# Weight-ring tiles 32 bytes longer, in a two-layer decoder trunk with PEER retrieval

## The chip, the cores and the metric

One core of a Trainium2 chip runs the whole program. The metric is the device time of one execution in microseconds (us); the time of the kernel before is the median of three runs.

## The reference, cut to what matters

512 tokens of width 1024 go through two layers. Each layer is a mixer (gated linear attention in the first, stick-breaking attention in the second, both beside attention into 256 memory tokens), an output projection, a layer norm, then the PEER block and another layer norm. The PEER block takes most of the time:

```python
q = (xf @ w_q).reshape(N, PEER_HEADS, 2, PEER_QHALF)
s = jnp.einsum('nhpd,hpkd->nhpk', q, subkeys)
# two rounds of top-16 give 128 of 16384 experts a token, and gates g
act = jax.nn.gelu(jnp.einsum('nd,nhkd->nhk', xt, u_tab[it]), approximate=False)
out = jnp.einsum('nhk,nhkd->nd', gt * act, v_tab[it])
```

## The kernel before, in words

**Precision.** Every fp32 operand of a projection is split into two tiles of type fp32r, a high part `hi` (a copy on ACT, L93) and the rest `lo` (a subtraction on DVE, L94). A product is then three matmuls. In `stat_mm` (L105 to L115) the weight block is the stationary operand and the activations `xhi`, `xlo` move: L113 is hi with xhi, L114 hi with xlo, L115 lo with xhi, for each of eight chunks of 128 rows. In `mov_mm` (L241 to L248) it is the other way round: the weight block moves, 512 columns at a time, past a stationary block of 128 x 128; L244, L246 and L248 each issue two matmuls.

**The PEER block** (`peer`, L943 on) has two long stages. For 384 of the 512 tokens all 16384 experts are computed densely; the other 128 tokens take their 128 experts by gathers.

- Stage 1 (L1336 to L1366; about 375 to 940 us, and 1880 to 2450 us in the second layer): for each of 128 blocks of `peer_u`, a DMA of 512 KB into `ur`, the split into `uh` and `ul`, 24 matmuls of 384 columns into `ph`, and a Gelu. Beside them run the selection of the experts on DVE (`Sel`), the one-hot gate matmuls into `pg` (L1259, L1260), the gathers of rows of `peer_u` on POOL's queue and their products on DVE (L1022).
- Stage 2 (L1420 to L1433; about 945 to 1440 us, and 2460 to 2950 us): for each of 128 blocks of `peer_v`, a DMA into `vr`, the split into `vh` and `vl`, the gate-weighted activation `w` (L1408) and its split into `whi` and `wlo` (L1411, L1412), and 18 matmuls of 512 columns into six accumulators: for each of three groups of 128 tokens, twice whi with vh, twice whi with vl, twice wlo with vh. Beside them run the gathers of `peer_v` and their sums on DVE (L1040).

Ahead of stage 1 the queries `pq` (16 blocks, L1310 to L1332) are made by `stat_mm` too. In both stages the order of work on PE, DVE and ACT is that of the program text (`manual_schedule`), and the side work is dealt out to the blocks by written costs in ns (`WB`, `GU`, `GR` and the others).

**Rings.** `split` takes its tiles from the pool `E.hl` (L59), three buffers of `hi` and three of `lo`, each 128 x 1024 fp32r, 4096 bytes in a partition. The raw blocks come from a ring of four (`RB`), and their loads are issued on SP's queue. `whi` and `wlo` have five buffers each (`TAIL`, L1406, L1407), 1536 bytes in a partition. Buffers of one name lie one behind the other, and the pools lie one behind the other in the order in which they are opened: const, xres, raw, hl, lnp, and then the pools of each part.

**Where the tiles lie.** In the compiled program of before, the byte at which a tile starts in its partition, modulo 128, is:

| tiles | start modulo 128 |
|---|---|
| `xhi`, `xlo` (pool xres, ahead of hl) | 64 |
| the six of hl (`uh`, `ul`, `vh`, `vl`, `anh` and the others): 87744, 91840, 95936 for hi, 100032, 104128, 108224 for lo | 64 |
| `whi` and `wlo`, ten tiles from 166336 on | 64 |
| `mhl`, the split memory tokens (mixer A) | 0 |
| mixer A's output projection: `woh`, `wol`, and `cat` but for chunks 4 and 5 | 96 |
| the same, chunks 4 and 5, which lie in `xhi` and `xlo` | 64 |
| mixer B's output projection, all of it | 64 |

All slices of these tiles that a matmul reads begin at multiples of 512 bytes.

Of the kernel before, what the change touches and what calls it, by code (L numbers as in the profile page):

```python
# [10 lines left out]
F32R = mybir.dt.float32r  # L11
# [5 lines left out]
P = 128  # L17
T = 512
NT = 4
D = 1024  # L20
# [10 lines left out]
def new_x(E):  # L31

    E.xhi = E.xp.tile([P, NC, T], F32R, tag="xhi", name="xhi")
    E.xlo = E.xp.tile([P, NC, T], F32R, tag="xlo", name="xlo")


def setup(ctx, tc):
# [19 lines left out]
    new_x(E)  # L57
    E.raw = ctx.enter_context(tc.tile_pool(name="raw", bufs=RB))
    E.hl = ctx.enter_context(tc.tile_pool(name="hl", bufs=3))  # L59
# [5 lines left out]
@contextmanager  # L65
def psum_pool(E, **tags):

    with E.tc.tile_pool(name="ps", bufs=1, space=bass.MemoryType.PSUM, reuse_waits="tile") as p:
        E.ps, old = (p, tags), getattr(E, "ps", None)
        yield  # L70
        E.ps = old


def psum(E, name="ps", tag="ps"):
    p, tags = E.ps
    return p.tile([P, 512], F32, tag=tag, name=name, bufs=tags[tag])


def load_raw(E, src, name):
    t = E.raw.tile([P, D], F32, tag="raw", name=name)  # L80
    E.last_load = E.nc.sync.dma_start(t, src)
    return t


def split(E, raw, name, pool=None, tag="", later=None, eng=None, rows=None):

    nc = E.nc
    eng = eng or nc.vector
    pool = pool or E.hl
    hi = pool.tile([P, D], F32R, tag=tag + "hi", name=f"{name}h")  # L90
    lo = pool.tile([P, D], F32R, tag=tag + "lo", name=f"{name}l")
    if rows is None:
        nc.scalar.activation(hi, raw, AF.Copy)  # L93
        sub = lambda: eng.tensor_sub(lo, raw, hi.bitcast(F32))  # L94
    else:
        nc.scalar.activation(hi, raw, AF.Copy, scale=rows)
        sub = lambda: eng.scalar_tensor_tensor(lo, raw, rows, hi.bitcast(F32), op0=ALU.mult, op1=ALU.subtract)
    if later is None:
        sub()
    else:  # L100
        later.append(sub)
    return hi, lo
# [525 lines left out]
def mixer_b(E, wst, wnat, wo, lng, lnb):  # L628
# [5 lines left out]
    with tc.tile_pool(name="bcat", bufs=1, reuse_waits="tile") as cp:  # L634
# [8 lines left out]
        with tc.tile_pool(name="mbx", bufs=1, reuse_waits="tile") as mp, tc.tile_pool(name="mbwk", bufs=2, reuse_waits="tile") as wk:  # L643
# [20 lines left out]
            def ev_stat(b, ps):  # L664
                if b >= 12:
                    dst = qm[:, b - 12]
                else:
                    dst = wk.tile([P, T], F32, tag=("kT", "qT")[b % 2], name="kq", bufs=1)
                    kq[b] = dst
                act.append(nc.scalar.activation(dst, ps, AF.Copy))  # L670
# [113 lines left out]
            with psum_pool(E, ps=2, z=4, c=2), tc.manual_schedule(engines={eng.PE, eng.DVE, eng.Activation}):  # L784
                parts = {}

                def prep(src, b):

                    raw = load_raw(E, src[b], "bs")
                    hi = E.hl.tile([P, D], F32R, tag="hi", name="bsh")  # L790
                    lo = E.hl.tile([P, D], F32R, tag="lo", name="bsl")
                    nc.scalar.activation(hi, raw, AF.Copy)
                    nc.gpsimd.tensor_sub(lo, raw, hi.bitcast(F32))
                    parts[b] = hi, lo

                def stat(b):
                    ps = psum(E, name="bsp")
                    stat_mm(E, ps, *parts.pop(b))
                    ev_stat(b, ps)

                vacc = []

                def values(u):

                    hi, lo = parts.pop(4 + u)
                    if u == 0:
                        vacc.extend(psum(E, name="bva") for _ in range(2))
                    for cc in range(4):
                        c = 4 * u + cc
                        h, l = hi[:, cc * 256:(cc + 1) * 256], lo[:, cc * 256:(cc + 1) * 256]  # L810
                        for t in range(NT):
                            xh, xl = E.xhi[:, c, t * P:(t + 1) * P], E.xlo[:, c, t * P:(t + 1) * P]
                            a = vacc[t // 2][:, t % 2 * 256:t % 2 * 256 + 256]
                            nc.tensor.matmul(a, xh, h, start=(c == 0 and t % 2 == 0), stop=False, skip_group_check=True)
                            nc.tensor.matmul(a, xh, l, start=False, stop=False, skip_group_check=True)
                            nc.tensor.matmul(a, xl, h, start=False, stop=(c == NC - 1), skip_group_check=True)

                prep(wst, 4)
                prep(wst, 5)
                for j in range(1, 6):  # L820
                    h, g = 2 * j, 2 * j - 2
                    phase1(h)
                    ln(h)
                    ln(h + 1)
                    phase3(g)
                    phase3(g + 1)
                    softplus(h)
                    softplus(h + 1)
                    if j < 5:
                        stat(h + 2)  # L830
                    else:
                        values(0)
                    sp_hi(h)
                    sp_hi(h + 1)
                    if j < 4:
                        prep(wst, h + 4)
                    elif j == 4:
                        prep(wnat, 4)
                    if j < 5:
                        stat(h + 3)  # L840
                    else:
                        values(1)
                        for k in range(2):
                            nc.scalar.activation(v[:, 2 * k:2 * k + 2, 512:], vacc[k].rearrange("p (t n) -> p t n", t=2), AF.Copy)
                    sp_lo(h)
                    sp_lo(h + 1)
                    if j < 4:
                        prep(wst, h + 5)
                    elif j == 4:
                        prep(wnat, 5)  # L850
                    phase4(j - 1)
                phase3(10)
                phase3(11)
                phase4(5)
# [58 lines left out]
TD = 384  # L913
# [23 lines left out]
LEAD = 3  # L937
TAIL = 5
RB = 4
SEG = [(0, 1, 0, 16, 16), (1, 1, 16, 8, 8), (2, 1, 24, 8, 5), (3, 1, 32, 8, 4), (4, 1, 40, 4, 3), (5, 3, 44, 4, 2), (8, 8, 56, 1, 1)]  # L940


def peer(E, mixer, wq, sk, ut, vt, un, lng, lnb, out_dram=None):  # L943
# [6 lines left out]
    with ExitStack() as pp:  # L950
# [97 lines left out]
        with ExitStack() as up:  # L1048
# [21 lines left out]
            class Sel:  # L1070
# [18 lines left out]
                def stage2(self, h):  # L1089

                    v = self.top_s[:, 2 * h:2 * h + 4].rearrange("p (h two) k -> p two h k", two=2)
                    for a, n, o, w, m in SEG:
                        dst = cand[:, :, o:o + n * w].rearrange("p h (a w) -> p h a w", a=n)[:, :, :, :m]
# [219 lines left out]
            for r in range(17):  # L1313
                if r < 16:
                    if r < LEAD:
                        pn = pes[r]
                    else:
                        hi, lo = parts.pop(r)
# [17 lines left out]
            for b in range(P + 1):  # L1336
# [7 lines left out]
                if b < P:  # L1344
                    if b > 0:
                        prep(b + 18, later)
                    hi, lo = parts.pop(16 + b)
# [22 lines left out]
        wv = pp.enter_context(tc.tile_pool(name="wv", bufs=2, reuse_waits="tile"))  # L1370
# [14 lines left out]
        def vprep(i):  # L1385
            if i >= P:
                return
            b = vorder[i]
            raw = load_raw(E, vt[b * P:(b + 1) * P], "vr")
            if i in gcuts:  # L1390
                g1 = gcuts[gcuts.index(i) + 1]
                if i == 0:
                    vp["g"] = g0
                else:
                    vp["g"] = E.xp.tile([P, NSUB, g1 - i, TS], F32, tag=("xhi", "xlo")[gcuts.index(i) % 2], name="gl")
                nc.sync.dma_start(vp["g"], Gd[:, :, b:b + g1 - i].rearrange("s p i n -> p s i n"))
                vp["i"] = i
            if b >= KB:
                av = keep[:, b - KB]
            else:  # L1400
                if b % AL == 0:
                    vp["a"] = wv.tile([P, AL, TD], F32, tag="al", name="al", bufs=3)
                    nc.sync.dma_start(vp["a"].rearrange("p (g a) n -> p g a n", a=AB), Ad[b // AB:b // AB + AL // AB].rearrange("g p a n -> p g a n"))
                av = vp["a"][:, b % AL]
            w = wv.tile([P, TD], F32, tag="w", name="w")
            whi = wv.tile([P, TD], F32R, tag="whi", name="whi", bufs=TAIL)  # L1406
            wlo = wv.tile([P, TD], F32R, tag="wlo", name="wlo", bufs=TAIL)  # L1407
            nc.vector.tensor_mul(w.rearrange("p (s n) -> p s n", s=NSUB), vp["g"][:, :, i - vp["i"]],  # L1408
                                 av.rearrange("p (s n) -> p s n", s=NSUB))
            hi, lo = split(E, raw, "v", wv if i >= P - (TAIL - 3) else None)  # L1410
            nc.scalar.activation(whi, w, AF.Copy)  # L1411
            nc.vector.tensor_sub(wlo, w, whi.bitcast(F32))  # L1412
            vp[i] = (whi, wlo, hi, lo)

        tail = []
        with tc.manual_schedule(engines={mybir.EngineType.DVE, mybir.EngineType.Activation, mybir.EngineType.PE}):
# [3 lines left out]
            for b in range(P):  # L1420
# [4 lines left out]
                whi, wlo, hi, lo = vp.pop(b)  # L1425
# [104 lines left out]
```

## Time and profile before

| | |
|---|---|
| median of 3 runs | 2988.55 us (2986.0 to 3000.78) |
| the profiled execution | 2996.65 us, its span 2994.9 us |
| granted TensorE clock, mean | 0.989 |
| PE busy | 2935.1 us (98% of the span), 16250 matmul records |
| weight loads (PEld) busy | 2591.7 us (87%) |
| DVE busy | 2401.1 us (80%) |
| ACT busy | 1428.3 us (48%) |
| POOL busy | 634.0 us (21%) |
| DMA | 789.91 MB, mean 264 GB/s |

Busy times are sums of the instructions' durations without overlap. Matmuls are pipelined, so the duration of one (342 ns for `ph`) is longer than the distance from its start to the next one's; the distances are read from the timeline. PEld is the queue of weight loads, which run beside matmuls.

### The profile page before, as it was taken

The page shows a single profiled execution, that of the slowest core. Times are in us where ns is not written, and L with a number is a line of the kernel's source. Part 1 is how long each engine was busy: PE and PEld are TensorE (multiplying, and loading weights), DVE is VectorE, ACT ScalarE, POOL GpSimd, SP SyncE. Part 2 cuts the span into 40 slices and gives each one's busy share as a digit, 9 for nine tenths or more (in the row PEclk, how much of TensorE's full clock was granted, in tenths as well). Part 3 has the DMA queues.
Part 4 walks back from the last instruction along what each step waited for, and adds up shares of the span by engine and source line. Part 5 has one row for each costly group of instructions (what it writes and reads, how often), then busy time and mean ns, then how long its engine had stood idle before and what let it go on. Part 6 is the DMA issues. An engine that isn't in the chain of part 4 may idle for free.

```text
span 2994.9 us, 44504 instructions
## 1 busy us (share of the span) xinstructions
PE 2935.1 (98%) x16250; PEld 2591.7 (87%) x16250; DVE 2401.1 (80%) x5301; ACT 1428.3 (48%) x2484; POOL 634.0 (21%) x560
## 2 busy tenths in 40 slices
PE   8999999999999999999999999999999999999998
PEld 7878899999998888888766788999999998888886
DVE  5555899999886888888856648999999778888888
ACT  5342357666674333333345513466676653333332
POOL 0100132221233222222002000321213233222220
PEclk9999999999999999999999989999999999999999
DMA  4331488889999999999411313789889999999995
GB/s 171 119 106 57 146 301 302 320 303 328 335 323 337 313 349 353 374 344 346 150 64 43 105 39 118 283 310 321 303 325 323 332 326 334 352 348 363 355 354 175
DMA packets 315131, 789.91 MB, mean 264 GB/s; under 512 B 41872, under 2 KB 134048, under 8 KB 308512
## 3 DMA queue, kind: packets, MB, share of 16 engines
q1 hardware_dynamic: 216960, 419.48, 41.0%
q0 software_dynamic: 73728, 268.47, 25.4%
q10 hardware_dynamic: 24224, 99.13, 8.4%
q8 instruction: 127, 2.08, 0.3%
q14 instruction: 92, 0.75, 0.1%
HBM read 692.09 MB, written 94.90 MB: 263 GB/s over the span
## 4 chain that ended last, share of the span: by engine, by line
PE 92%; DVE 5%; issue 1%; DMA 1%; ACT 1%; DVEq 0%; ACTq 0%; SPq 0%
PE ph L113 11%; PE acc L244 11%; PE acc L246 11%; PE ph L115 11%; PE ph L114 11%; PE acc L248 11%; PE pq L114 2%; PE pq L115 2%; PE pq L113 2%; PE pg L1259 1%; PE pg L1260 1%; PE pss L1307 1%; PE oacc L246 1%; PE oacc L248 1%; PE oacc L244 1%
## 5 line engine op out<-in xcount | busy, mean ns | idle before, releaser
L113 PE MATMUL ph<-xhi,uh 128*128 128x384 f32 x2048 | 701.4, 342 | 0.0
L115 PE MATMUL ph<-xhi,ul 128*128 128x384 f32 x2048 | 686.7, 335 | 0.2
L114 PE MATMUL ph<-xlo,uh 128*128 128x384 f32 x2048 | 686.0, 335 | 0.0
L93 ACT ACTIVATE vh<-vr 128x1024 fp32r<-128x1024 f32 x256 | 271.4, 1060 | 604.0 <-issue 455.8
L987 POOL DMA_INDIRECT gr<-in_un,gidx x256 | 302.7, 1182 | 1032.6 <-DVE gr L1022 807.4
L244 PE MATMUL acc<-vh,whi 128*128 128x512 f32 x1536 | 474.7, 390 | 8.3 <-ACT whi L1411 8.3
L246 PE MATMUL acc<-vl,whi 128*128 128x512 f32 x1536 | 474.5, 390 | 0.0
L248 PE MATMUL acc<-vh,wlo 128*128 128x512 f32 x1536 | 473.7, 390 | 0.4 <-DVE wlo L1412 0.4
L94 DVE TENSOR_TENSOR vl<-vr,vh 128x1024 fp32r<-128x1024 f32 x256 | 313.4, 1224 | 169.2 <-ACT vh L93 168.8
L987 POOL DMA_INDIRECT gr<-in_vt,gidx x256 | 279.8, 1093 | 773.5 <-DVE va L1040 664.0
L93 ACT ACTIVATE uh<-ur 128x1024 fp32r<-128x1024 f32 x288 | 304.6, 1058 | 245.8 <-PE ph L114 234.4
L94 DVE TENSOR_TENSOR ul<-ur,uh 128x1024 fp32r<-128x1024 f32 x288 | 350.4, 1217 | 74.2 <-ACT uh L93 72.7
L114 PEld LDWEIGHTS ph<-xlo,uh 128*128 128x128 f32 x2048 | 386.4, 189 | 0.0
L115 PEld LDWEIGHTS ph<-xhi,ul 128*128 128x128 f32 x2048 | 385.5, 188 | 0.9 <-DVE ul L94 0.9
L113 PEld LDWEIGHTS ph<-xhi,uh 128*128 128x128 f32 x2048 | 386.0, 188 | 0.0
L244 PEld LDWEIGHTS acc<-vh,whi 128*128 128x128 f32 x1536 | 288.0, 188 | 70.2 <-ACT whi L1411 10.8
L248 PEld LDWEIGHTS acc<-vh,wlo 128*128 128x128 f32 x1536 | 288.2, 188 | 61.6 <-DVE wlo L1412 2.0
L246 PEld LDWEIGHTS acc<-vl,whi 128*128 128x128 f32 x1536 | 288.3, 188 | 61.4 <-DVE vl L94 1.8
L1040 DVE SCALAR_TENSOR_TENSOR va<-gr,gw,va 128x1024 f32<-128x1024 f32 x254 | 325.1, 1280 | 12.6 <-DMA gr<-in_vt,gidx 12.4
L1022 DVE SCALAR_TENSOR_TENSOR gr<-gr,xnat 128x1024 f32<-128x1024 f32 x256 | 310.2, 1214 | 16.4 <-DMA gr<-in_un,gidx 16.4
L1232 ACT ACTIVATE obl<-obh,rat 128x128 f16<-128x128 f16 x768 | 244.3, 393 | 20.8 <-ACT gt L1263 5.2
L1411 ACT ACTIVATE whi<-w 128x384 fp32r<-128x384 f32 x256 | 130.7, 511 | 46.0 <-DVE w L1408 45.9
(332 smaller groups left out, 4165.0 us busy)
## 6 DMA issues: line engine op xcount, KB each, us to landing
ur<-in_ut SPq DMA_DIRECT2D x256, 512.0 KB
vr<-in_vt SPq DMA_DIRECT2D x256, 512.0 KB
Gd<-gt ACTq DMA_DIRECT2D x48, 1024.0 KB
gl<-Gd SPq DMA_DIRECT2D x30, 1536.0 KB
Ad<-act ACTq DMA_DIRECT2D x108, 384.0 KB
al<-Ad SPq DMA_DIRECT2D x108, 384.0 KB
ur<-in_wq SPq DMA_DIRECT2D x32, 512.0 KB
bs<-in_b_st SPq DMA_DIRECT2D x14, 512.0 KB
```

What stands on the lines that cost most here:

```text
L93: nc.scalar.activation(hi, raw, AF.Copy)
L94: sub = lambda: eng.tensor_sub(lo, raw, hi.bitcast(F32))
L113: nc.tensor.matmul(ps, h, xhi[:, c, sl], start=(c == 0), stop=False)
L114: nc.tensor.matmul(ps, h, xlo[:, c, sl], start=False, stop=False)
L115: nc.tensor.matmul(ps, l, xhi[:, c, sl], start=False, stop=(c == NC - 1))
L244: nc.tensor.matmul(acc[hf], lh, hi[:, hf * 512:(hf + 1) * 512], start=first, stop=False)
L246: nc.tensor.matmul(acc[hf], lh, lo[:, hf * 512:(hf + 1) * 512], start=False, stop=False)
L248: nc.tensor.matmul(acc[hf], ll, hi[:, hf * 512:(hf + 1) * 512], start=False, stop=last)
L987: nc.gpsimd.indirect_dma_start(out=gr, out_offset=None, in_=tab, in_offset=bass.IndirectOffsetOnAxis(ap=gidx[:, k:k + 1], axis=0))
L1022: nc.vector.scalar_tensor_tensor(gr, gr, 1.0, E.x[:, 0], op0=ALU.mult, op1=ALU.mult, accum_out=gh[:, k:k + 1])
L1040: nc.vector.scalar_tensor_tensor(va, gr, gw[:, k:k + 1], va, op0=ALU.mult, op1=ALU.add)
L1232: nc.scalar.activation(obl[:, q], obh[:, q], AF.Copy, scale=rat[:, n0 + q:n0 + q + 1])
```

## The change

The tiles of the pool hl that hold split weights become 1024 + 8 elements long instead of 1024, and those of `whi` and `wlo` 384 + 8 instead of 384; each use takes the first 1024 or 384 of them. Eight elements are 32 bytes. No instruction is added, removed or moved, and no shape that an instruction sees is changed. Tiles that `split` takes from another pool keep their length.

```diff
@@ split
-    hi = pool.tile([P, D], F32R, tag=tag + "hi", name=f"{name}h")
-    lo = pool.tile([P, D], F32R, tag=tag + "lo", name=f"{name}l")
+    w = D + PAD if pool is E.hl else D
+    hi = pool.tile([P, w], F32R, tag=tag + "hi", name=f"{name}h")[:, :D]
+    lo = pool.tile([P, w], F32R, tag=tag + "lo", name=f"{name}l")[:, :D]
@@ mixer_b, prep
-                    hi = E.hl.tile([P, D], F32R, tag="hi", name="bsh")
-                    lo = E.hl.tile([P, D], F32R, tag="lo", name="bsl")
+                    hi = E.hl.tile([P, D + PAD], F32R, tag="hi", name="bsh")[:, :D]
+                    lo = E.hl.tile([P, D + PAD], F32R, tag="lo", name="bsl")[:, :D]
@@ constants
 RB = 4
+PAD = 8
@@ peer, vprep
-            whi = wv.tile([P, TD], F32R, tag="whi", name="whi", bufs=TAIL)
-            wlo = wv.tile([P, TD], F32R, tag="wlo", name="wlo", bufs=TAIL)
+            whi = wv.tile([P, TD + PAD], F32R, tag="whi", name="whi", bufs=TAIL)[:, :TD]
+            wlo = wv.tile([P, TD + PAD], F32R, tag="wlo", name="wlo", bufs=TAIL)[:, :TD]
```

## Rows read from the trace of the kernel before

**Rows 1.** The page's chain that ended last, shares of the span by engine

```profile
PE 92%; DVE 5%; issue 1%; DMA 1%; ACT 1%; DVEq 0%; ACTq 0%; SPq 0%
```

**Rows 2.** Busy time by stretch; columns as in the first line

```profile
core 0: us, PE busy (x) PEld busy (x) DVE busy (x) ACT busy (x) POOL busy (x), PEclk, DMA share, GB/s
450.00:525.00 75.00, 75.00 (x520) 72.64 (x519) 72.65 (x230) 53.00 (x122) 15.28 (x17) 1.00 0.89 306
...
750.00:850.00 100.00, 100.00 (x676) 97.45 (x675) 83.69 (x165) 70.14 (x145) 29.30 (x25) 1.00 0.93 333
...
1100.00:1200.00 100.00, 100.00 (x443) 82.81 (x442) 82.71 (x99) 35.48 (x49) 24.26 (x24) 1.00 1.01 354
...
1960.00:2040.00 80.00, 80.00 (x549) 77.64 (x548) 77.66 (x246) 57.33 (x129) 15.92 (x17) 1.00 0.87 303
```

**Rows 3.** Groups of instructions, PE: busy us, mean ns, idle before

```profile
L113 PE MATMUL ph<-xhi,uh 128*128 128x384 f32 x2048 | 701.4, 342 | 0.0
...
L244 PE MATMUL acc<-vh,whi 128*128 128x512 f32 x1536 | 474.7, 390 | 8.3 <-ACT whi L1411 8.3
...
L113 PE MATMUL pq<-xhi,uh 128*128 128x512 f32 (+2 forms) x304 | 116.1, 382 | 1.0 <-ACT xhi L870 1.0
```

**Rows 4.** Timeline of stage 1, one block: start us, us, engine, line

```profile
701.84 0.33 PE L113 MATMUL ph<-xhi,uh 128*128 128x384 f32 x1
701.85 0.19 PEld L114 LDWEIGHTS ph<-xlo,uh 128*128 128x128 f32 x1
...
704.79 0.34 PE L115 MATMUL ph<-xhi,ul 128*128 128x384 f32 x1
```

**Rows 5.** Timeline of stage 2, PE; x2 is two matmuls from that start

```profile
1201.75 0.61 PE L244 MATMUL acc<-vh,whi 128*128 128x512 f32 x2
...
1208.55 0.61 PE L244 MATMUL acc<-vh,whi 128*128 128x512 f32 x2
```

**Rows 6.** Timeline of mixer A, PE: values projection, 256 columns

```profile
120.06 0.28 PE L170 MATMUL ana<-anh,xhi 128*128 128x256 f32 x1
...
125.70 0.28 PE L172 MATMUL ana<-anh,xlo 128*128 128x256 f32 x1
```

**Rows 7.** Timeline of mixer A, PE: three stretches of memory keys and values

```profile
62.67 0.28 PE L113 MATMUL mkp<-mhl,mkh 128*128 128x256 f32 x1
...
67.86 0.28 PE L115 MATMUL mkp<-mhl,mkl 128*128 128x256 f32 x1
...
68.33 0.28 PE L170 MATMUL mva<-mvh,mhl 128*128 128x256 f32 x1
...
73.31 0.28 PE L172 MATMUL mva<-mvh,mhl 128*128 128x256 f32 x1
...
90.31 0.28 PE L113 MATMUL mkp<-mhl,mkh 128*128 128x256 f32 x1
...
92.58 0.28 PE L115 MATMUL mkp<-mhl,mkl 128*128 128x256 f32 x1
```

**Rows 8.** Timeline of mixer A's output projection, PE

```profile
229.81 0.63 PE L244 MATMUL oacc<-woh,xhi 128*128 128x512 f32 x2
...
232.60 1.03 PE L866 MATMUL xtp<-ident,xnat 128*128 128x128 f32 x8
...
236.26 0.61 PE L244 MATMUL oacc<-woh,cat 128*128 128x512 f32 x2
...
241.25 0.62 PE L248 MATMUL oacc<-woh,cat 128*128 128x512 f32 x2
```

**Rows 9.** Waits of DVE, 400 to 900 us: total, times, longest

```profile
DVE obh L1243 <- PE pg L1260: 21.4, 10, 3.7
```

**Rows 10.** Two lines on DVE: duration ns min/median/max

```profile
L204 DVE TENSOR_TENSOR mhl<-memr,mhl x2: 1222/1224/1227, 41.9 to 46.5; 128x1024 fp32r<-128x1024 f32 x2
...
L94 DVE TENSOR_TENSOR vl<-vr,vh x256: 1215/1225/1227, 940.7 to 2968.9; 128x1024 fp32r<-128x1024 f32 x128
```

**Rows 11.** Stage 2: a wait of ACT, 960 to 1430 us, and one stretch's DMA

```profile
ACT vh L93 <- DMA vr<-in_vt: 10.7, 4, 4.5
...
1230.00:1240.00 10.00, 10.00 (x46) 8.29 (x45) 7.11 (x9) 3.56 (x6) 1.93 (x3) 1.00 1.04 401
```

## The prediction, made before the changed kernel was run

> **What bounds the kernel now.** I read the chain of waits first: 92% of the span is PE [rows 1]. The busy time by stretch shows the same for both long stages: PE is busy for all of each stretch, at a granted clock of 1.00 [rows 2]. So the time is the number of matmuls times the distance from one start to the next. The groups give the numbers: 3 x 2048 = 6144 matmuls of 384 columns in stage 1, 3 x 1536 = 4608 of 512 in stage 2, 3 x 304 = 912 for the queries [rows 3]. The second thing to see is what stands close behind PE: DVE, busy 72.65 of 75 us (97%) in the first half of stage 1 and 97% again in the second layer, and the DMA engines in stage 2, with a share of 1.01 [rows 2].
>
> **The distance holds a surplus.** In the timeline of stage 1 eighteen matmuls start between 701.84 and 704.79 us: 2.95 / 17 = 173.5 ns [rows 4]. In stage 2 thirty take 1208.55 - 1201.75 = 6.80 us: 226.7 ns [rows 5]. In a projection of 256 columns 48 starts span 5.64 us: 120.0 ns [rows 6]. From 256 to 384 and from 384 to 512 columns the distance grows by 53.4 ns, 0.417 ns a column, one cycle of 2.4 GHz. What is left over is the same at all three widths: 120.0 - 106.7 = 13.3 ns a matmul. Over 6144 + 4608 matmuls that is 143 us, and it is all this change can reach.
>
> **Is the surplus one of place?** While a matmul runs, the weights of the next one load: that load starts 0.01 us after the matmul [rows 4]. Call d the place of the moving operand less that of the weights loading beside it, modulo 128 bytes, from the table of places. In rows 4 to 6 all lie at 64, so d = 0. Two spots have another d:
> - Memory keys and values, mhl at 0 and the ring at 64: d = 64. Two stretches run at 4.98 / 44 = 113.2 and 2.27 / 20 = 113.5 ns, surplus 6.6; a third, with the same places, at 5.19 / 44 = 118.0, surplus 11.3 [rows 7].
> - Chunks 4 and 5 of mixer A's output projection, moving at 96 and weights at 64: d = 32. Twelve matmuls take 232.60 - 229.81 = 2.79 us, 232.5 ns, surplus 19.2. The chunks with both operands at 96 take 4.99 / 22 = 226.8 ns, surplus 13.5 [rows 8].
>
> So the common place does not matter (64 or 96), the difference does: 13.3 ns at d = 0, 19.2 at 32, 6.6 to 11.3 at 64. No row has d = 96. Its ends are 0 (nothing left over) and 19.2 (the worst seen). I take 3: if each spot and the one half a turn away share the same total, then d = 96 has (13.3 + 9) - 19.2 = 3.1, with 9 the middle of the two values at 64. This value carries the forecast.
>
> The Trainium skill says otherwise ("TensorE: Matmul & The Clock Gate", Step-by-step): TensorE has two read ports, and loading the next weights takes no bandwidth from the running matmul. By that rule rows 6 and 7, equal in width, would be equal, and the change would give 0 us; the trace has 120.0 against 113.2 ns.
>
> **The change, part by part.** A tile of 4128 bytes is 32 x 128 + 32, so neighbours step by 32. The ring's hi tiles come to 64, 96, 0 and its lo tiles to 32, 64, 96; all behind the ring moves by 6 x 32 = 192, that is 64 modulo 128. whi then starts at 0: 0, 32, 64, 96, 0, and wlo at 32, 64, 96, 0, 32.
>
> *Stage 1.* xhi and xlo stay at 64. Of a block's 24 matmuls 16 have a hi tile loading beside them and 8 a lo tile. By buffer that is d = 0 (16) and 32 (8); 96 (16) and 0 (8); 64 (16) and 96 (8). Over 72 matmuls: 24 at 0, 8 at 32, 16 at 64, 24 at 96. Mean surplus (24 x 13.3 + 8 x 19.2 + 16 x 9 + 24 x 3) / 72 = 9.6 ns, 3.7 less than 13.3. Times 6144: 23 us.
>
> *Queries.* The same pattern; 768 of the 912 have 384 columns or more: 3 us.
>
> *Stage 2.* Both operands vary. In six matmuls the pairs (moving, loading) are hi with whi three times, then lo with whi, lo with wlo, hi with wlo; the rings of 3 and 5 meet in 15 ways. Of 90 cases 22 are at 0, 21 at 32, 24 at 64, 23 at 96: mean 10.9 ns, 2.4 less. Times 4608: 11 us.
>
> *Mixer A's chunks 4 and 5.* woh and wol move to 32, xhi stays: d from 32 to 96, 96 matmuls x 16 ns = 1.5 us. Other projections of the mixers, with d of all four kinds, some with the roles turned round: 2 us at most.
>
> *What lies beside.* The split on ACT and DVE writes to other places. DVE's subtraction takes 1224 ns with a target at 0 and 1225 at 64 [rows 10]: nothing. The gather buffers move by 64 bytes; no row has them elsewhere; I take nothing, since transfers hold up ACT for only 10.7 us in 470 [rows 11], and if a gather got slower stage 2 would show it first. No wait, instruction or DMA is added.
>
> *What keeps of it.* PE gains 24 x 3.7 = 90 ns in a block of about 4.6 us, 1.9%. DVE has 3% idle there, part of it in waits for PE's gate matmuls, 21.4 us in 500, which shrink along [rows 9]; late next would be ul, on DVE. I count 0.8 of the gain in the half where DVE is full and all of it in the other: 20 us. In stage 2 the DMA engines must deliver 1.1% more than 354 GB/s; a stretch at 401 shows that they can [rows 2, 11], but the share is 1.0 on average, so 0.8 again: 9 us. Sum 20 + 3 + 9 + 1.5 + 1 = 34.5 us.
>
> The profiled execution takes 2996.65 us, 8.1 above the median, without a stage that looks disturbed; I take the gain off the median: 2988.55 - 34.5 = 2954.
>
> **Rivals.**
> - *All of it.* d = 96 leaves nothing over and d = 64 the smaller 6.6: the mean surplus is 8.0 in stage 1 and 9.5 in stage 2; 5.3 x 6144 + 3.8 x 4608 = 50 us, with the queries and mixers 57, if DVE and DMA follow: 2932. For it: 6.6 stands in two of three stretches.
> - *DVE or DMA becomes the bound.* Of 34.5 us half is given back in waits for ul and vr: 2971. For it: 97% and 1.01 in rows 2; against it: DVE's remaining idle time exceeds what is asked.
> - *Place changes nothing.* The odd distances in rows 7 and 8 come from what else those stretches do; the surplus is that of each weight load. Then 2988.5. Against it: rows 6 and 7 are matmuls of the same width and type in the same mixer, and rows 8 differ within one accumulation, where only the chunk changes. This is what the rule of the Trainium skill above would give.
> - *Slower: d = 96 is as bad as 32.* Its place is hi of the second buffer and lo of the third in stage 1, a third of all its matmuls. At 19.2 there and 11.3 at 64 the mean is 15.5 in stage 1 and 15.7 in stage 2: 2.2 x 6144 + 2.4 x 4608 = 25 us more, with the queries 26: 3015. It decides from a surplus of 14 ns at d = 96 on, where stage 1 comes out even. For it: d = 32 is 6 ns worse than d = 0, and 96 is the same distance the other way; against it: 32 and 96 would then share 38 ns where 0 and 64 share 22.
>
> **How the numbers follow.** A measurement of this kernel can tell about 0.5%, 15 us, from no change. Chances: the forecast 0.58, all of it 0.10, DVE or DMA as bound 0.12 (half of it still over 0.5%), nothing 0.11, slower 0.09. Faster by over 0.5%: 0.58 + 0.10 + 0.06 = 0.74; within: 0.11 + 0.06 = 0.17; slower: 0.09. The range runs from the whole gain, 2932, a little lower for the blocks left out, to a gain of 6 us, where d = 96 leaves 12: 2929 to 2983. That leaves out the slower case and most of "nothing".
>
> **What would show it.** In the timeline of stage 1 the distance should differ by block in a cycle of three: one block near 175 ns on average (d = 0 and 32), two near 167. In stage 2 it should vary within a block with a period of 15 blocks. Over a stretch of stage 2 without waits the count of matmuls in 100 us should rise from 443 to about 448. DVE's share in the first half of stage 1 should rise to 98 or 99%, and its wait for the gate matmuls fall. If the distances stay at 173.5 and 226.7 whatever the buffer, the reason is wrong; if they fall and the span does not, look for PE waiting on ul or whi.

## The result: slower by 1.1%

| | before | after |
|---|---|---|
| median of 4 runs each | 2989.78 us (2986.0 to 3000.78) | 3023.78 us (3022.96 to 3025.74) |
| span of the profiled execution | 2994.9 us | 3021.2 us |
| PE busy | 2935.1 us | 2962.2 us |

The ratio is 1.0108, its 95% interval 1.0083 to 1.0134: 34 us more, where 34.5 us less was forecast. The time lies outside the range, on the side of the rival that was given 0.09.

### The profile after

The page's busy times and its chain by engine, against [rows 1]:

```profile
PE 2962.2 (98%) x16250; PEld 2591.5 (86%) x16250; DVE 2402.2 (80%) x5301; ACT 1428.3 (47%) x2484; POOL 628.2 (21%) x560
...
PE 91%; DVE 5%; issue 1%; DMA 1%; ACT 1%; DVEq 0%; ACTq 0%; SPq 0%
```

The chain is the same, PE from end to end; the same 16250 matmuls take it 27 us longer, and DVE, ACT and the weight loads are as busy as before. The same four stretches as in [rows 2]:

```profile
core 0: us, PE busy (x) PEld busy (x) DVE busy (x) ACT busy (x) POOL busy (x), PEclk, DMA share, GB/s
450.00:525.00 75.00, 75.00 (x511) 72.80 (x511) 72.16 (x229) 53.25 (x121) 14.99 (x16) 1.00 0.85 296
750.00:850.00 100.00, 100.00 (x661) 97.61 (x660) 85.16 (x164) 69.04 (x142) 30.00 (x25) 1.00 0.91 331
1100.00:1200.00 100.00, 100.00 (x433) 80.95 (x432) 80.63 (x96) 35.23 (x49) 24.05 (x25) 1.00 0.99 346
1960.00:2040.00 80.00, 80.00 (x534) 77.87 (x533) 74.79 (x232) 54.60 (x118) 16.98 (x18) 1.00 0.86 301
```

PE has no gap in any of them and its granted clock is still 1.00, yet the count falls: 443 to 433 in 100 us of stage 2, 520 to 511 in the first half of stage 1. The DMA engines move less per second, as a PE that asks later would have it. So each matmul starts later after the one before. In the timeline of stage 1, the second and the last matmul of three successive blocks, one in each buffer of the ring (compare [rows 4]):

```profile
703.03 0.34 PE L115 MATMUL ph<-xlo,uh 128*128 128x384 f32 x1
...
706.88 0.34 PE L116 MATMUL ph<-xhi,ul 128*128 128x384 f32 x1
...
707.75 0.34 PE L115 MATMUL ph<-xlo,uh 128*128 128x384 f32 x1
...
711.61 0.34 PE L116 MATMUL ph<-xhi,ul 128*128 128x384 f32 x1
...
712.48 0.33 PE L115 MATMUL ph<-xlo,uh 128*128 128x384 f32 x1
...
716.34 0.33 PE L116 MATMUL ph<-xhi,ul 128*128 128x384 f32 x1
```

Twenty-two distances a block: 3.85, 3.86 and 3.86 us, 175.0 to 175.5 ns in every buffer. Before it was 173.5; the forecast had 175, 167, 167 in turn. In stage 2 (compare [rows 5]):

```profile
1201.72 0.63 PE L245 MATMUL acc<-vh,whi 128*128 128x512 f32 x2
...
1208.69 0.63 PE L245 MATMUL acc<-vh,whi 128*128 128x512 f32 x2
```

Thirty matmuls take 6.97 us, 232.3 ns, against 226.7. Chunks 4 and 5 of the output projection, whose difference the change moves from 32 to 96 modulo 128 (compare [rows 8]):

```profile
234.86 0.61 PE L247 MATMUL oacc<-wol,cat 128*128 128x512 f32 x2
...
241.22 0.62 PE L245 MATMUL oacc<-woh,xhi 128*128 128x512 f32 x2
...
243.54 0.63 PE L249 MATMUL oacc<-woh,xlo 128*128 128x512 f32 x2
```

Up to 241.22 moving tile and weights start at the same place: 6.36 / 28 = 227.1 ns. Behind it, at 96 modulo 128 (224 modulo 256): 2.32 / 10 = 232.0 ns, where 3 ns of surplus (216 ns) were forecast.

The waits behind which the forecast had set a limit, DVE's for the gate matmuls [rows 9] and ACT's for the next block of values [rows 11]:

```profile
DVE obh L1245 <- PE pg L1262: 22.9, 9, 3.7
```

```profile
ACT vh L94 <- DMA vr<-in_vt: 23.4, 7, 4.6
```

The first is as before. The second is 13 us longer, but it doesn't reach PE. Two of PE's groups, as in [rows 3]:

```profile
L114 PE MATMUL ph<-xhi,uh 128*128 128x384 f32 x2048 | 704.9, 344 | 0.0
...
L245 PE MATMUL acc<-vh,whi 128*128 128x512 f32 x1536 | 483.9, 396 | 8.5 <-ACT whi L1413 8.4
```

PE's idle time in front of the accumulation is still 8.5 us; what grew is the matmul itself, by 2 ns at 384 columns and 6 at 512.

**Where the 34 us are.** In what follows a distance is the mean over all neighbouring matmuls of one group in the trace, pauses (over 40 ns above the columns' own time) left out: 5,770 pairs in stage 1, 4,560 in stage 2. Stage 1 went from 173.5 to 175.3 ns, stage 2 from 226.7 to 232.0, the queries of 512 columns from 227.3 to 231.9. Over 4608 matmuls stage 2 loses 5.3 x 4608 = 24.4 us; its two passes, from first to last start, grew from 532.5 and 527.2 to 545.4 and 539.7 us, 25.4 together. Stage 1 loses 1.8 x 6144 = 11 us in distances, of which 3.1 in each pass shows (587.2 to 590.3): shorter pauses give the rest back. What lies ahead of the first stage 1 is 1.1 us longer, and the work between the layers 6.3 shorter (393.2 to 386.9). Sum 1.1 + 6.2 + 25.4 - 6.3 = 26.4, the 26.3 by which the spans differ. The missing 8 us to the medians belong to the kernel before, whose profiled execution was 7 us above its median: in experiments 11 and 12, whose long stages take about as long as before, the work between the layers took 384.4 and 385.8. The 6.3 us are no gain of the change either. The stretch from 1700 to 1880 us lies in that work, before and after:

```profile
1700.00:1880.00 180.00, 175.63 (x865) 152.41 (x866) 122.83 (x493) 55.74 (x79) 8.97 (x8) 0.93 0.33 112
```

```profile
1700.00:1880.00 180.00, 172.19 (x904) 143.71 (x904) 118.75 (x457) 55.75 (x79) 6.35 (x6) 1.00 0.30 103
```

In the trace of before the granted clock is 0.5 (1.2 GHz) for 20.5 us from 1767 us on, with PE busy 25.8 of the 27 us ahead of it; after, it is 1.00 in the whole stretch. The prediction took that trace for one "without a stage that looks disturbed".

### The profile page after: what moved, and what is told of

Its sections match the earlier page's. It is cut to its first block, busy times and chain, and to the rows that moved or that the text cites. A ratio compares the mean times of both kernels' runs of the same rounds, so it can differ in the third digit from the quotient of the medians.

```text
span 3021.2 us, 44504 instructions
## 1 busy us (share of the span) xinstructions
PE 2962.2 (98%) x16250; PEld 2591.5 (86%) x16250; DVE 2402.2 (80%) x5301; ACT 1428.3 (47%) x2484; POOL 628.2 (21%) x560
## 4 chain that ended last, share of the span: by engine, by line
PE 91%; DVE 5%; issue 1%; DMA 1%; ACT 1%; DVEq 0%; ACTq 0%; SPq 0%
PE ph L114 11%; PE acc L245 11%; PE acc L249 11%; PE acc L247 11%; PE ph L115 11%; PE ph L116 11%; PE pq L115 2%; PE pq L116 2%; PE pq L114 2%; PE pg L1261 1%; PE pg L1262 1%; PE pss L1309 1%; PE bsp L114 1%; PE bsp L115 1%; PE bsp L116 1%
## 5 line engine op out<-in xcount | busy, mean ns | idle before, releaser
L245 PE MATMUL acc<-vh,whi 128*128 128x512 f32 x1536 | 483.9, 396 | 8.5 <-ACT whi L1413 8.4
L249 PE MATMUL acc<-vh,wlo 128*128 128x512 f32 x1536 | 483.0, 395 | 0.0
L247 PE MATMUL acc<-vl,whi 128*128 128x512 f32 x1536 | 481.8, 395 | 0.0
L245 PEld LDWEIGHTS acc<-vh,whi 128*128 128x128 f32 x1536 | 289.1, 189 | 79.1 <-ACT whi L1413 11.1
L1265 ACT ACTIVATE gt<-pg 128x512 f32<-128x512 f32 x192 | 114.1, 594 | 81.1 <-PE pg L1262 42.8
```

The costliest lines, as they stand in the source:

```text
L245: nc.tensor.matmul(acc[hf], lh, hi[:, hf * 512:(hf + 1) * 512], start=first, stop=False)
L247: nc.tensor.matmul(acc[hf], lh, lo[:, hf * 512:(hf + 1) * 512], start=False, stop=False)
L249: nc.tensor.matmul(acc[hf], ll, hi[:, hf * 512:(hf + 1) * 512], start=False, stop=last)
```

## The experiments

The first theories: **D**, the price of a matmul depends on the difference between its moving operand and the weights that load beside it, modulo 128, pair by pair, as the prediction had it, only with a dearer value at 96; **M**, what is dear is the mixture, operands that step from place to place. The later ones, **U**, **C** and **H**, stand in the expectations.

### 1. The ring alone

Against the changed kernel:

```diff
-whi = wv.tile([P, TD + PAD], F32R, tag="whi", name="whi", bufs=TAIL)[:, :TD]
-wlo = wv.tile([P, TD + PAD], F32R, tag="wlo", name="wlo", bufs=TAIL)[:, :TD]
+whi = wv.tile([P, TD], F32R, tag="whi", name="whi", bufs=TAIL)
+wlo = wv.tile([P, TD], F32R, tag="wlo", name="wlo", bufs=TAIL)
```

> Only the weight ring is longer; whi and wlo keep 1536 bytes and lie at 0. Theory M (mixture: the 13.3 ns surplus is that of a steady rhythm which holds only while successive matmuls meet the same places; as soon as the places change from one matmul to the next the distance rises to about 175.4 ns at 384 columns and 231 to 232 ns at 512): stage 1 as in the changed kernel, 175.4 ns, and stage 2 also near 231 ns, since vh and vl still vary; time 25 to 35 us over the kernel before. Theory D (the surplus of each matmul follows from its own difference of places, with 96 as bad as 32): in stage 2 a third of the matmuls keeps d = 64 and a sixth d = 0, so 229 ns or less on average, and the distance differs by block; 18 to 24 us over before.

3028.52 us against 2993.81, ratio 1.0117 (1.0079 to 1.0155). Stage 1 175.3 ns and stage 2 232.7: the ring alone, the moving operand of stage 2, costs as much as the whole change. M had 231 to 232 ns for stage 2 and comes close; D had 229 or less and missed.

### 2. The gate-weighted tiles alone

Against the changed kernel, and so at the two places in mixer B:

```diff
-w = D + PAD if pool is E.hl else D
+w = D
```

> Only whi and wlo are longer; the ring stays at 64. Both theories: stage 1 exactly as before, 173.5 ns. Theory M: stage 2 near 231 ns instead of 226.7, 4608 x 4.5 = 20 us over the kernel before. Theory D: the four differences in about equal parts, with the same mean as in the changed kernel, the distance differing by block with the place of whi. If a third cause were at work (the pools behind the ring lying 64 bytes further on), neither stage would change: 0 us.

3010.45 us, ratio 1.0049 (1.0025 to 1.0073). The busy times by stretch, PE alone:

```profile
750.00:850.00 100.00, 100.00 (x675) 1.00 0.94 338
1100.00:1200.00 100.00, 100.00 (x432) 1.00 0.98 344
```

Stage 1, untouched, is as before (173.5 ns, 675 matmuls against 676); stage 2 is at 232.0 ns. So the two halves of the change don't add up in stage 2: either one brings the whole loss. D and M both allow that.

### 3. The same change with 128 bytes

Against the changed kernel:

```diff
-PAD = 8
+PAD = 32
```

> The same edit with 128 bytes instead of 32, so that all places modulo 128 stay at 64. Theories M and D: distances of 173.5 and 226.7 ns, the time of the kernel before within 0.3%. Rival (the longer tiles cost by themselves, or the places count modulo 256 or 512): 15 to 35 us slower, as the changed kernel is.

3020.44 us, ratio 1.0087 (1.0057 to 1.0118); 175.6 and 231.0 ns. All operands now start at the same place modulo 128, so neither D nor M, which count modulo 128, can make a difference, and yet nearly the whole loss is there. Either the places count modulo more than 128, or longer tiles cost by themselves; experiments 6 and 8, where the tiles keep their length, and 11 decide for the first.

### 4. One constant shift of the ring

From here on the edits are against the kernel before:

```diff
     new_x(E)
+    E.fill = E.xp.tile([P, 16], F32, name="fill")
```

No tile is longer; everything behind the resident activations moves by 64 bytes. Stage 1 has one constant difference, 192 modulo 256, stage 2 has 0 throughout.

> No tile is longer; one unused tile of 64 bytes stands between xhi, xlo and everything behind them, so that xhi and xlo lie at 64 and the ring, whi and wlo all at 0. Stage 1 and the queries then run at a constant difference of 64, stage 2 at 0. Theory M: constant places keep a rhythm, and that at 64 leaves 6.6 to 11.3 ns as in the memory projections, so 166.6 to 171.3 ns in stage 1: 14 to 45 us faster, less what DVE holds back; stage 2 at 226.7. Rival: the low distances at 64 belong to 256 columns only, and any unequal place costs, as in the changed kernel: 175 ns, 10 to 13 us slower.

3005.02 us, ratio 1.0045 (1.0019 to 1.007). Stage 2 stays at 226.7 ns, though every place in it moved: the place itself is nothing. Stage 1 rises to 174.9, the queries of 512 columns to 233.3. Only projections of 256 columns fall, the values projection of rows 6 (`ana`) from 120.0 to 115.6 ns. This is where the forecast's d = 64 came from, and the wider matmuls don't share it. No operand steps here, so stepping isn't needed for a loss.

### 5 to 8. Constant differences, four at a time

Two fillers set two constant differences, for stage 1 and for stage 2:

```diff
     new_x(E)
+    E.fill = E.xp.tile([P, F1 // 4], F32, name="fill")
...
         vp = {}
+        vp["fill"] = wv.tile([P, F2 // 4], F32, tag="fill", name="fill2", bufs=1)
```

F1 and F2 in bytes are 32 and 96, 128 and 192, 160 and 32, 224 and 128.

> No operand tile is longer than before. A filler tile of 32 bytes behind the resident transposed activations moves the ring and all behind it, and one of 96 bytes ahead of the gate-weighted tiles moves those again: stage 1 has every moving operand 224 (mod 256) behind the weights that load beside it, stage 2 160 (mod 256), both constant over the whole stage. So unequal places are had without any change of place. Theory U (the surplus of 13.3 ns belongs to places that agree modulo 256, and a constant unequal difference costs as much as a mixed one): 384 columns 174.5 to 176.0 ns, accumulation of stage 2 230 to 234 ns. Rival C (what costs is that the difference changes from one matmul to the next; a constant one is at the old price or under it): 384 columns at most 173.5, accumulation at most 226.8. Rival H (the price falls with the distance from a meeting place, so differences near half a period are best): stage 2 below 226, stage 1 above 174.

> Fillers of 128 and 192 bytes: constant differences of 128 (mod 256) in stage 1 and of 64 (mod 256) in stage 2. Theory U: 174.5 to 176.0 ns at 384 columns, 230 to 234 ns in the accumulation; with 5,770 and 4,560 matmuls that is a span 25 to 45 us above the kernel before. Rival C: at most 173.5 and 226.8, a span of about 2995 or under. Rival H: half a period (128) is the best place, so stage 1 falls below 172 ns, and stage 2 at 64 lies between. A rival on the size of the period (it is 128 and the earlier run with pads of 128 bytes was slow for its changing places): 128 gives 173.5 as before.

> Fillers of 160 and 32 bytes: constant differences of 96 (mod 256) in stage 1 and 224 in stage 2. Theory U: 174.5 to 176.0 ns at 384 columns, 230 to 234 ns in the accumulation. Rival C: at most 173.5 and 226.8. Rival H: 96 is next to half a period, so stage 1 is below 173 and stage 2 (224, 32 away from equal) the worst of all, at least 232.

> Fillers of 224 and 128 bytes: constant differences of 32 (mod 256) in stage 1 and 128 in stage 2. Theory U: 174.5 to 176.0 ns at 384 columns, 230 to 234 ns in the accumulation. Rival C: at most 173.5 and 226.8. Rival H: stage 2 at half a period falls below 224, and stage 1 at 32 is above 175; the span is then under that of the kernel before. The value that a forecast from short runs of the kernel before gave for a difference of 32 was 19.2 ns of surplus, so 179 ns at 384 columns, whatever the period.

One run each: 3027.67, 3016.62, 3045.97 and 3025.9 us, with the kernel before at 2984.64 beside them; what follows rests on the distances in the traces. The stretch 1100 to 1200 us of stage 2, PE alone, in the first, second, third and fourth:

```profile
1100.00:1200.00 100.00, 100.00 (x429) 1.00 0.98 343
```

```profile
1100.00:1200.00 100.00, 100.00 (x439) 1.00 0.99 351
```

```profile
1100.00:1200.00 100.00, 100.00 (x430) 1.00 0.98 345
```

```profile
1100.00:1200.00 100.00, 100.00 (x431) 1.00 0.98 343
```

Before it was 443. With no operand stepping at all, a difference of 160, 64, 224 or 128 slows stage 2 to 234.2, 228.9, 233.3 and 232.8 ns. C (only a changing difference costs) falls, and so does H (half a period is best). U holds at 512 columns, though 64 is a little cheaper than it said. At 384 it fits one of four and nearly a second: 128 and 96 gave 176.0 and 176.6 ns, while 224 and 32 gave 173.6 and 173.8. The 179 ns that the forecast's price for 32 would give was not seen. In the third, a block of stage 1:

```profile
703.80 0.34 PE L115 MATMUL ph<-xlo,uh 128*128 128x384 f32 x1
...
707.69 0.33 PE L116 MATMUL ph<-xhi,ul 128*128 128x384 f32 x1
```

3.89 / 22 = 176.8 ns, at 96, the value that carried the forecast.

The mean of 173.8 in the fourth hides two distances. A block of stage 1 in the first layer and one in the second, with the same difference of 32:

```profile
705.73 0.33 PE L115 MATMUL ph<-xlo,uh 128*128 128x384 f32 x1
...
709.54 0.34 PE L116 MATMUL ph<-xhi,ul 128*128 128x384 f32 x1
...
2352.54 0.34 PE L115 MATMUL ph<-xlo,uh 128*128 128x384 f32 x1
...
2356.42 0.34 PE L116 MATMUL ph<-xhi,ul 128*128 128x384 f32 x1
```

3.81 / 22 = 173.2 and 3.88 / 22 = 176.4 ns. Of the 256 blocks 215 run at 173.3 ns on average and 41 at 176.6, the last 37 of the second layer among them, and the queries of 384 columns at 176.7. Experiments 4 (131 blocks at 173.2, 121 at 176.7) and 10 (235 at 173.3, 21 at 176.5) show the same two levels. So at 384 columns the difference of places doesn't settle the distance by itself; what picks the level isn't shown.

### 9 and 10. The last differences, and a step of 256 bytes

Fillers F1 of 192 and 96 bytes; the gate-weighted tiles 64 elements longer, in the second used from the 16th byte on:

```diff
-whi = wv.tile([P, TD], ..., bufs=TAIL)
+whi = wv.tile([P, TD + 64], ..., bufs=TAIL)[:, :TD]        # 9, wlo alike
+whi = wv.tile([P, TD + 64], ..., bufs=TAIL)[:, 4:4 + TD]   # 10, wlo alike
```

> A filler of 192 bytes gives stage 1 a constant difference of 64 (mod 256), the last but one of its row; and the gate-weighted tiles get the change under study at 256 bytes instead of 32, so that successive buffers differ by 256 and every difference in stage 2 stays 0 modulo 256. Theory U with a period of 256: the accumulation stays at 226.7 ns, as in the kernel before, and its two stages at 532 and 527 us. Rival (any longer tile is slow, or the period is longer than 256): 230 to 233 ns, each stage 10 to 15 us longer. Stage 1 at 64: theory U says 174 to 177 ns; if 64 is a good place, as it was the least bad for 512 columns (228.9), under 173 ns, which would be worth some 4 us a stage.

> A filler of 96 bytes gives stage 1 a constant difference of 160 (mod 256), the last one of its row; the gate-weighted tiles are 256 bytes longer and used from their 16th byte on, so that stage 2 has a constant difference of 240, half of the finest step so far. Theory U: stage 1 174 to 177 ns; stage 2 between 230 and 234, since only equal places are special. Rival (what counts is a unit of 32 or 64 bytes, so that 16 bytes within it change nothing): stage 2 at 226.7. Rival (equal places are a meeting that a small offset breaks): under 226.

One run each: 2989.34 and 3022.53 us, the kernel before 2983.9. The stretch of stage 2 in the first and in the second:

```profile
1100.00:1200.00 100.00, 100.00 (x443) 1.00 0.99 354
```

```profile
1100.00:1200.00 100.00, 100.00 (x430) 1.00 0.99 345
```

Steps of 256 bytes from buffer to buffer cost nothing: 226.8 ns, passes of 531.9 and 526.4 us. An offset of 16 bytes costs the full price, 233.2 ns. At 384 columns 64 is harmless in every block, 160 in 235 of 256; a block of the first:

```profile
703.98 0.34 PE L115 MATMUL ph<-xlo,uh 128*128 128x384 f32 x1
...
707.79 0.34 PE L116 MATMUL ph<-xhi,ul 128*128 128x384 f32 x1
```

3.81 / 22 = 173.2 ns. U had 174 to 177 for both and missed, and so did the guess of under 173 for 64.

### 11. The second experiment with 256 bytes

```diff
-whi = wv.tile([P, TD], ..., bufs=TAIL)
+whi = wv.tile([P, TD + 64], ..., bufs=TAIL)[:, :TD]        # wlo alike
```

> The edit of the run that padded the gate-weighted tiles alone (ratio 1.0049), with 256 bytes in place of 32 and nothing else. The tiles get longer and the memory tighter as there, and only the places modulo 256 stay equal. Theory U: accumulation at 226.7 ns, ratio between 0.998 and 1.002. Rival (longer tiles cost by themselves, by their strides or by what lies behind them): ratio 1.004 to 1.006, accumulation at 232.

2991.93 us against 2995.93, ratio 1.0001 (0.998 to 1.0021); 226.7 ns. Longer gate-weighted tiles by themselves cost nothing. With the second experiment this settles it: the same edit loses 0.5% with 32 bytes and nothing with 256.

### 12. The best constant places

```diff
     new_x(E)
+    E.fill = E.xp.tile([P, 48], F32, name="fill")
```

> Only a filler of 192 bytes behind the resident activations: differences of 64 (mod 256) in stage 1, 0 in stage 2. It is the best of the constant places found, 173.3 ns at 384 columns against 173.5, with stages of 585.0 us against 587.2 each; against that stand about 1,100 matmuls of 512 columns in the projections at 229 instead of 227.3 (2 us) and some 260 at 233 instead of 228 (1.4 us). Expected: 0 to 4 us less than the kernel before, ratio 0.998 to 1.001, so no gain that could be told. Rival (the accumulation loses again through the shifted places, as it did when they changed): above 1.004.

2992.32 us against 2995.93, ratio 0.9991 (0.9973 to 1.001): no difference that could be told. No version found beats the kernel before.

### The prices together

The surplus over 0.417 ns a column, by difference modulo 256, each from a kernel in which that difference is constant (384 columns: stage 1; 512: stage 2 or, for 32, 96 and 192, the queries; 256: the values projection of mixer A, `ana`):

| difference | 0 | 32 | 64 | 96 | 128 | 160 | 192 | 224 |
|---|---|---|---|---|---|---|---|---|
| 256 columns, ns | 13.3 | 10.0 | 8.9 | 13.3 | 11.9 | 10.7 | 8.9 | 11.6 |
| 384 columns, ns | 13.5 | 13.8 | 13.3 | 16.6 | 16.0 | 13.6 | 14.9 | 13.6 |
| 512 columns, ns | 13.4 | 20.1 | 15.6 | 19.9 | 19.5 | 21.0 | 20.0 | 20.0 |

At 512 columns other matmuls with the same difference agree with the row to 2 ns. At 384 the values at 32, 160 and 192 are means of blocks at about 13.3 and about 16.6. At 256 other projections with a difference of 64 or 192 had 6.7 to 11.1 ns where `ana` has 8.9: two rates at the same places, as [rows 7] had already shown.

In stage 2 of the changed kernel 591, 687, 694, 607, 525, 392, 515 and 553 matmuls have these differences in turn. Weighted so, the last row gives 213.3 + 18.5 = 231.8 ns; 232.0 was measured. The ring alone comes to 232.3 by the same count (measured 232.7), the gate-weighted tiles alone to 231.8 (232.0). So in these three kernels the loss in stage 2 is the mean of the prices, to 0.4 ns. With 128 bytes it is not: the count gives 229.7 ns where 231.0 was measured, 1.3 of a loss of 4.3 left over. In stage 1 the same count gives 174.5 where 175.3 was measured, and with 128 bytes 174.6 where it was 175.6: half of that rise is left over. Nor is the price kept pair by pair within a mixture: pairs at difference 0 ran at 231.2 ns in stage 2 of the changed kernel, and at 175.4 in stage 1. What a matmul costs there depends on its neighbours too, and how is open.

## Why the prediction was wrong

- **PE is the bound, the sum is count times distance:** right. The loss is in the distances, at a full clock; neither DVE nor the DMA engines decided anything, and the limits set for them (0.8 of the gain) were never tried.
- **The surplus is a matter of relative place:** right at 512 columns; at 384 it is not the whole of it, as the two distances at one difference show. Experiments 4 and 9 move every place of stage 2 and leave its distance alone, 5 to 8 move one operand against the other and change it by up to 7.5 ns. The rival that place changes nothing is refuted by them. The Trainium skill ("TensorE: Matmul & The Clock Gate", Step-by-step) says that the streaming operand and the weight load have independent read ports and that the load takes no bandwidth from the running matmul. What the prediction drew from that rule, that place changes nothing, does not hold: a stream and a load of unchanged shapes ran at 226.7 or at 234.2 ns by their places alone.
- **The step that failed** is the price list, "13.3 ns at d = 0, 19.2 at 32, 6.6 to 11.3 at 64", with 3 taken for 96. It had four faults. The sentence "the same at all three widths" was shown for d = 0 only, and the value at 64 came from matmuls of 256 columns [rows 7]; there it is 8.9, as taken, but 13.3 at 384 and 15.6 at 512. The two stretches of the same matmuls in [rows 7], 113.5 and 118.0 ns at the same places, were averaged, though they showed that place alone did not fix the distance there. The value at 96, by a half-turn rule that no row bore out, is 13.3, 16.6 and 19.9 by width, not 3. And the differences were taken modulo 128: modulo 256 a difference of 128, priced as 0, costs 16.0 and 19.5. The value at 32 is the one that held, at the width of its rows [rows 8]: 20.1 against 19.2; at 384 columns it is 13.8 on average, of blocks at 13.3 and 16.6.
- **Stage 1, 23 us gained, and stage 2, 11 us gained:** instead 6 and 25 us lost. The terms turn over because at 512 columns every difference but 0 is dearer, and at 384 none is cheaper by more than 0.2 ns. No version tried was faster than the kernel before by an amount that could be told.
- **Queries, 3 us, and chunks 4 and 5, 1.5 us:** the queries lose 4.6 ns a matmul at 512 columns; the chunks stay at 232 ns, since 32 and 224, the differences that they have modulo 256 before and after, cost the same at 512 columns (20.1 and 20.0).
- **The rival on the slower side** named the deciding point, a surplus of over 14 ns at 96, and it was met but for one price: 96 costs 16.6 at 384 columns and 19.9 at 512, and 224, the same place modulo 128, 13.6 and 20.0. Its 3015 is 9 us short, as it left 64 and 128 cheap. It was argued away by "32 and 96 would then share 38 ns where 0 and 64 share 22": a symmetry for which there were no rows. At 512 columns 32 and 96 do share 40.
- **What would show it** worked as named: no cycle of three by block, and the count in stage 2 went from 443 to 433, not to 448.

## What to carry to other kernels

Before operand tiles of fp32r matmuls are padded or a pool in front of them changes size, list where moving operands and weights start modulo 256 bytes: in these runs equal places gave 226.7 ns at 512 columns, every other constant difference tried 229 to 234, and 16 bytes were enough; a pad of 256 bytes on the gate-weighted tiles cost nothing (ratio 1.0001). A price read at one width stands for that width only, and a value that no row has should not carry a forecast when a single step of a symmetry is all that gives it: here the range should have reached 19 ns for it, the worst value seen, as its stated end already said.

## What the runs showed that was not expected

- Moving operand and loading weights interact, with a period of 256 bytes: 0 and 256 alike (226.7 ns), 128 not (232.8).
- The sign depends on the width: at 256 columns unequal places in `ana` are cheaper by up to 4.4 ns (120.0 to 115.6; at 96 nothing), at 512 dearer by 2 to 8, at 384 between nothing and 3.
- At 384 columns a matmul at unchanged places runs at one of two distances, 173.3 or 176.7 ns, and keeps to one almost always for a whole block, often for many: differences of 32, 160 and 192 show both within one run, 0, 64 and 224 stay near the first, 96 at the second.
- At 512 columns the differences other than 0 cost about the same, 19.5 to 21 ns, save 64 with 15.6. By this row, the finer the places are spread, the nearer the mean comes to the dear value.
- Which reads meet, and why a pair at equal places is slower among unequal ones, isn't shown. In the kernels with constant differences a matmul's own weights and those that load beside it share a place, so the two can't be told apart there.
